# One priority number of the mixer from 40000 to 15000, and the longer lag one attention unit earlier

## The chip, the cores and the metric

The kernel runs on one core of a Trainium2 chip. The metric is the device time of one launch in microseconds (us). The launch before takes 2202.68 us (median of 3 runs, 2202.24 to 2213.45). Five engines run at the same time, each through its own list of instructions in a fixed order: TensorE (PE, matrix multiplications), VectorE (DVE), ScalarE (ACT), GpSimd (POOL) and SyncE (SP), whose list is almost only the start of transfers. An instruction that waits holds up all that stands behind it in its list. 16 DMA engines move the data.

## The reference, cut to what matters

Two layers with shared weights run over 128 context tokens and 512 latent tokens, 640 columns in one tile of 642. The reference computes, for each layer:

```
h = rmsnorm(x) * (1 + scale1) + shift1                  # modulated by c or c_ctx
aq, ak, av, bq, bk, bv, cz, cx, cb, cc, cdt, du = split(h @ w_in)
ya = diff_attention(aq, ak, av)       # 4 heads, two softmaxes each, subtracted
yb = gqa_attention(bq, bk, bv)        # 4 query heads on 2 key heads
yc = ssd_mixer(cz, cx, cb, cc, cdt)   # bidirectional state space scan in chunks of 128
yd = s5_mixer(du)                     # bidirectional complex diagonal scan, then a GLU
y  = concat(ya, yb, yc, yd) @ w_out
x  = x + gate1 * rmsnorm(y)
g, v = split(dwconv(h2 @ w_up));  x = x + gate2 * rmsnorm((silu(g) * v) @ w_down)
```

Keys, values and scan states of the context are outputs too. The four mixers of a layer do not depend on one another; each needs only its own columns of `h @ w_in`.

## The kernel before, in words

Activations lie with features on the 128 partitions and tokens in the columns. Every float32 product is made of three matmuls on parts rounded to float32r (`lin3`: high x high, high x low, low x high), over the token spans 0 to 256 and 256 to 642. A projection of 128 features is 8 chunks x 3 matmuls x 2 spans = 48 matmuls.

A layer has a mixer stage (`mixer`) and an FFN stage (`ffn`). The mixer emits, in this order of code: the first four projections (`first_proj`: du0, du1, aq0, ak0); the rest in the order of the string `ORD` (V for values and dt; bk, cz, bq, cx, aq1, ak1, cb, cc; each Q step normalises, rotates and stores queries or keys to DRAM); `ssd_steps`; `s5` (the S5 recurrence, in four quarters, each with tables `s_tb` and `s_to` loaded from DRAM into a single buffer); `s5_glu`; `ssd`; `attention`; and `w_out` in two parts. In layer 0 the modulation weights of later stages (`adaln`, tile `wm`) run between them.

What sets the order in each engine's list is not the order of the code. Each part is emitted under a priority (`self.prio`, from the table `PR`), and the scheduler takes, among the instructions that are ready by its own reckoning, the one with the smallest number. Before, the order of the numbers in a mixer is: s5 0, glu 10000, attn 20000, ssd 30000, proj 40000, st 55000, w_out 61000 and 62000. Layer 1 adds 1000000. The list of every engine is then fixed; on the chip it runs in that order whatever comes late.

`attention` has six units: heads 0 and 1 of the first differential pair, one GQA unit with two query heads, the same again. A unit is a list of (front, back) pairs. A front makes scores (`pse<-k,q`), takes maxima on DVE and exponentials on ACT (tile `at_p`, 4 buffers). A back turns the weights on PE (`psu<-identr,at_p`), splits them (`at_h`, `at_l`) and multiplies them with the values (`psv<-v,at_h`). `waiting` holds the backs that lag behind their fronts. From the fourth unit on, the weights alternate between two pools, the second of which (`au`) takes the memory that `ssd` gives back.

`ssd` needs the projections cx0, cx1, cb and cc, convolved (`cf`), and the memory of the S5 and query-key tiles, so it comes after `s5_glu`. Names in rows: `s_tb`, `s_to` S5 tables; `s_yh<-s_gs` matmuls are the GLU; `sd_...` and `cf` the SSD; `at_...` attention; `d_aq`, `d_bq`, `d_bk` queries and keys in DRAM, `q` and `k` the same loaded for a unit; `wr<-in_w_in` projection weights; `wm` modulation weights. The projections write the PSUM tile `psp` from `hh`, `hl` (activations) and `wh`, `wl` (weights).

Of the kernel before, what the change touches and what calls it, by code (L numbers as in the profile page):

```python
# [33 lines left out]
LAG = 1  # L34
# [2 lines left out]
SB = "vu"  # L37
WX = 8
XP = 0
PR = {"proj": 40000, "s5": 0, "glu": 10000, "ssd": 30000, "attn": 20000, "f0": 60000, "f1": 61000, "tab": 50000, "st": 55000, "lead": 299000, "wg": 165000, "norm": 300000, "first": 310000}  # L40
WP = (61000, 62000)
MID = 6
NTMP = (("nsr", TW - SPLIT, 2), ("nsr", TW - SPLIT, 2))
# [29 lines left out]
class K:  # L73
# [1272 lines left out]
    def attention(self, l, pool, kq):  # L1346

        self.attn_begin(l, pool)
        units = ((0, 0, 0), (0, 0, 1), (1, 0), (0, 1, 0), (0, 1, 1), (1, 1))
        waiting, new = [], self.attn_unit(l, pool, kq, *units[0])  # L1350
        self.tb, self.work = itertools.cycle("u"), itertools.cycle([pool])
        with ExitStack() as more:
            for i in range(len(units)):
                if i == 3:
                    self.tb = itertools.cycle("ud")
                    self.work = itertools.cycle([pool, more.enter_context(self.pool(f"au{l}", "right"))])
                items, new = new, self.attn_unit(l, pool, kq, *units[i + 1]) if i + 1 < len(units) else None
                for front, back in items:
                    front()
                    waiting.append(back)  # L1360
                    if len(waiting) > LAG + (i > 2):
                        waiting.pop(0)()
            for back in waiting:
                back()
# [20 lines left out]
    def ffn_first(self, l, pool, yp):  # L1385
# [4 lines left out]
        with self.pool(f"wx{l}", "right", NFIRST - 4 if WPL else 4) as wx:  # L1390
            self.leading([(self.a["w_up"][l, j], self.put(r, j % 2)) for j, r in enumerate(first)],
                         lambda i: self.pss(tags[i]), wx, 1000000 * l + PR["lead"], pool if WPL else None)
        return first
# [86 lines left out]
    def mixer(self, l, base, fill):  # L1480

        self.qd = {}
        with ExitStack() as left, ExitStack() as early:
# [8 lines left out]
            pb = proj.enter_context(self.pool(f"pj{l}"))  # L1492
            with self.pool(f"ld{l}", bufs=2) as lead, self.prio(base + PR["proj"]):
                raw = self.first_proj(l, pb, lead)
            pc = proj.enter_context(self.pool(f"pc{l}"))
            qk = early.enter_context(self.pool(f"qk{l}", "right"))
            with self.prio(base + PR["proj"]):
                sp = early.enter_context(self.pool(f"s5{l}", "right"))
                raws = {"aq0": raw[0], "ak0": raw[1]}
                self.cf = {}  # L1500
                for op in ORD.split():
# [13 lines left out]
                    else:  # L1515
                        for t in self.cz:
                            self.silu2(self.raw(pb), t, t)
            with self.prio(base + PR["st"]):
                self.ssd_steps(pb)
            with self.prio(base + PR["s5"]):  # L1520
                ys = self.s5(l, sp, pb)
            fill(0, base + PR["f0"])
            with self.prio(base + PR["glu"]):
# [287 lines left out]
```

## Time and profile before

| | us |
|---|---|
| median of 3 runs | 2202.68 (2202.24 to 2213.45) |
| the profiled execution, own time | 2191.5 |
| its span, first to last instruction | 2189.7 |
| layer 0: first S5 matmul to GLU / GLU to end of SSD | 153.5 / 122.7 |
| layer 1: first S5 matmul to GLU / GLU to end of SSD | 137.2 / 184.5 |
| attention after the SSD and first part of w_out: layer 0 / layer 1 | 118.5 / 122.0 |

The durations all come from the one profiled execution. Its own time is 11.2 us under the median of the runs, so a difference worked out in it is set against 2191.5 and then carried over to 2202.7. A stage is read by how long it lasts and by how busy PE, DVE and the transfers are in it; "granted clock" is the share of TensorE's 2.4 GHz that it was given on average, 0.5 being the lower level of 1.2 GHz.

### The profile page before, as it was taken

The numbers are of one execution on the slowest core, as the hardware profiler recorded it, in microseconds if no ns is written. First come the engines' busy times: TensorE is split into PE (matmuls) and PEld (weight loads), VectorE is DVE, ScalarE is ACT, GpSimd is POOL, SyncE is SP. The second block draws the span as 40 slices with busy tenths as digits, with TensorE's granted clock in tenths as the row PEclk, the third lists the DMA queues.
The fourth block names the chain that finished last, engine by engine and source line by source line (L and its number), as shares of the span: only waits on it lengthen the run. The fifth ranks groups of instructions, "written<-read, shape, count | busy, mean of one in ns | idle before, by whom it ended". The sixth has DMA issues, their size and how long they took to land.

```text
span 2189.7 us, 33260 instructions
## 1 busy us (share of the span) xinstructions
PE 1956.1 (89%) x12812; PEld 1786.6 (82%) x12812; DVE 1245.6 (57%) x2879; ACT 802.4 (37%) x1614; POOL 676.4 (31%) x723
## 2 busy tenths in 40 slices
PE   5996789999699999999988797897985999999997
PEld 2895775876597888999988786876875999999996
DVE  6876785475768575233366475653847631323345
ACT  3423353443452223232343244442444533313241
POOL 3553424200433352122244232323104332212232
PEclk9997789888799999999988887886866999999998
DMA  7464325134305665222224521310112012222221
GB/s 295 136 207 160 114 74 177 40 101 131 107 20 185 197 223 190 85 77 73 91 79 149 184 98 61 117 45 10 51 40 95 20 56 80 73 82 70 75 87 49
DMA packets 93511, 230.29 MB, mean 105 GB/s; under 512 B 17960, under 2 KB 30888, under 8 KB 93352
## 3 DMA queue, kind: packets, MB, share of 16 engines
q1 hardware_dynamic: 82856, 213.46, 29.8%
q10 hardware_dynamic: 10496, 14.71, 1.9%
q8 instruction: 101, 1.65, 0.3%
q14 instruction: 58, 0.48, 0.1%
HBM read 192.21 MB, written 35.92 MB: 104 GB/s over the span
## 4 chain that ended last, share of the span: by engine, by line
PE 67%; DVE 15%; DMA 9%; ACT 3%; issue 2%; POOL 2%; SPq 1%; ACTq 0%; POOLq 0%; DVEq 0%
PE psb L81 34%; PE psp L81 12%; PE psd L81 7%; PE pse L81 6%; PE psv L81 5%; DMA s_tb<-s5td 2%; DMA wm<-in_w_mod 1%; DVE nt L391 1%; PE psu L1209 1%; DMA wr<-in_w_down 1%; DVE x L394 1%; DMA ck<-in_cache_ak 1%; DVE wl L98 1%; DMA q<-d_bq 1%; DVE at_s L1279 1%
## 5 line engine op out<-in xcount | busy, mean ns | idle before, releaser
L81 PE MATMUL psb<-hh,wh 128*128 128x256 f32 (+1 forms) x1152 | 359.1, 312 | 2.3 <-DVE cv L451 2.3
L81 PE MATMUL psb<-hl,wh 128*128 128x256 f32 (+1 forms) x1152 | 358.3, 311 | 0.0
L81 PE MATMUL psb<-hh,wl 128*128 128x256 f32 (+1 forms) x1152 | 357.3, 310 | 0.0
L98 POOL TENSOR_TENSOR wl<-wr,wh 128x1024 fp32r<-128x1024 f32 (+3 forms) x87 | 192.3, 2211 | 502.7 <-ACT wh L95 451.6
L95 ACT CAST wh<-wr 128x1024 fp32r<-128x1024 f32 (+3 forms) x174 | 168.6, 970 | 417.9 <-PE psb L81 283.4
L81 PEld LDWEIGHTS psb<-hh,wh 128*128 128x128 f32 x1152 | 217.9, 189 | 13.3 <-issue 8.2
L81 PE MATMUL psp<-hh,wh 128*128 128x386 f32 (+1 forms) x640 | 215.3, 337 | 10.7 <-ACT hh L374 7.8
L81 PEld LDWEIGHTS psb<-hl,wh 128*128 128x128 f32 x1152 | 218.7, 190 | 3.4 <-issue 3.4
L81 PEld LDWEIGHTS psb<-hh,wl 128*128 128x128 f32 x1152 | 218.1, 189 | 3.4 <-issue 3.4
L81 PE MATMUL psp<-hl,wh 128*128 128x386 f32 (+1 forms) x640 | 209.8, 328 | 0.1
L81 PE MATMUL psp<-hh,wl 128*128 128x386 f32 (+1 forms) x640 | 207.0, 324 | 0.3 <-POOL wl L98 0.3
L98 DVE TENSOR_TENSOR wl<-wr,wh 128x1024 fp32r<-128x1024 f32 (+3 forms) x87 | 100.1, 1151 | 144.0 <-ACT wh L95 143.6
L81 PE MATMUL psb<-uh,wh 128*128 128x256 f32 (+1 forms) x544 | 169.9, 312 | 0.0
L81 PE MATMUL psb<-ul,wh 128*128 128x256 f32 (+1 forms) x544 | 169.4, 311 | 0.0
L81 PE MATMUL psb<-uh,wl 128*128 128x256 f32 (+1 forms) x544 | 169.1, 311 | 0.0
L81 PE MATMUL pse<-k,q 96*128 96x128 f32 (+5 forms) x288 | 107.1, 436 | 44.6 <-ACT at_p L1195 15.1
L81 PEld LDWEIGHTS psp<-hh,wh 128*128 128x128 f32 x640 | 129.0, 202 | 17.4 <-ACT hh L374 8.8
L81 PEld LDWEIGHTS psp<-hl,wh 128*128 128x128 f32 x640 | 129.3, 202 | 2.6 <-issue 1.1
L81 PEld LDWEIGHTS psp<-hh,wl 128*128 128x128 f32 x640 | 128.6, 201 | 1.4 <-issue 0.5
L1419 POOL TENSOR_TENSOR cv<-cv,cv 128x642 f32<-128x642 f32 x44 | 71.6, 1629 | 170.5 <-DVE cv L451 141.2
L81 PEld LDWEIGHTS pse<-k,q 96*128 96x128 f32 (+2 forms) x288 | 60.5, 229 | 77.7 <-issue 32.5
L450 DVE SCALAR_TENSOR_TENSOR cv<-psb,vec,cv 128x641 f32<-128x641 f32 x72 | 63.5, 881 | 103.2 <-ACT cv L449 103.2
(525 smaller groups left out, 4741.7 us busy)
## 6 DMA issues: line engine op xcount, KB each, us to landing
wm<-in_w_mod SPq DMA_DIRECT2D x96, 512.0 KB
wr<-in_w_up SPq DMA_DIRECT2D x88, 512.0 KB
wr<-in_w_in SPq DMA_DIRECT2D x30, 512.0 KB
wr<-in_w_down SPq DMA_DIRECT2D x32, 384.0 KB
wr<-in_w_down SPq DMA_DIRECT2D x32, 320.0 KB
wr<-in_w_out SPq DMA_DIRECT2D x16, 512.0 KB
s_tb<-s5td SPq DMA_DIRECT2D x8, 992.0 KB
s_to<-s5td SPq DMA_DIRECT2D x8, 768.0 KB
```

The costliest lines, as they stand in the source:

```text
L81: self.nc.tensor.matmul(out, w, x, start=start, stop=stop)
L95: nc.scalar.copy(hv, rv)
L98: e.tensor_sub(lv, rv, hv.bitcast(F32))
L391: nc.vector.scalar_tensor_tensor(t, y[c][:, t0:t1], gg[:, c, g:g + 1], r(t0, t1), op0=ALU.mult, op1=ALU.mult)
L394: (nc.gpsimd if c % 2 else nc.vector).tensor_add(xs, xs, t)
L450: nc.vector.scalar_tensor_tensor(out[:, 1:TW], x[:, 0:TW - 1], w[:, 0:1], out[:, 1:TW], op0=ALU.mult, op1=ALU.add)
L1209: nc.tensor.transpose(ps[:, 128 * j:128 * j + 128], s, self.c("ident"))
L1279: V.reduce_max(s[:, k:k + 1], ps, axis=AX.X)
L1419: G.tensor_mul(cv[0], cv[0], cv[1])
```

## The change

```
-PR = {"proj": 40000, "s5": 0, "glu": 10000, "ssd": 30000, "attn": 20000, ...}
+PR = {"proj": 15000, "s5": 0, "glu": 10000, "ssd": 30000, "attn": 20000, ...}
...
                     front()
                     waiting.append(back)
-                    if len(waiting) > LAG + (i > 2):
+                    if len(waiting) > LAG + (i > 1):
                         waiting.pop(0)()
```

The first line gives the projections a smaller number than attention; before, they had a larger one than attention and SSD. The second lets the third unit (index 2, GQA) keep two backs behind its fronts, as units four to six do already, in place of one. Nothing is computed differently; the FFN stages keep their order. The lists of the engines change in both mixers.

PE in layer 1, where the SSD begins. `psp<-hh..,hl..` with `wh`, `wl` at 128x386 are the last matmuls of a projection, `at_o` and `at_pp` belong to attention, `cf` to the SSD. Before:

```order
L81 MATMUL psp<-hh_96,wl 128x386
L81 MATMUL psp<-hh_100,wh 128x386
L81 MATMUL psp<-hl_101,wh 128x386
L81 MATMUL psp<-hh_100,wl 128x386
L1321 MATMUL psu<-identr,at_o 128x128
L1209 MATMUL psu<-identr,at_pp 128x128
L966 MATMUL psd<-identr,cf_12768 128x128 x5
L81 MATMUL psu<-v,at_h 128x128
L81 MATMUL psu<-v,at_l 128x64
L966 MATMUL psd<-identr,cf_12934 128x128 x5
```

The last three of the projections are in one block of 144 matmuls straight before these rows, and 240 matmuls of projections stand behind the first GLU matmul. The same place in the changed kernel, 19 rows behind the last GLU matmul:

```order
L81 MATMUL psp<-hh_100,wl 128x386
L1209 MATMUL psu<-identr,at_p 128x128 x4
L81 MATMUL pse<-k,q 128x128 x4
L81 MATMUL pse<-k,q 128x512
L966 MATMUL psd<-identr,cf_12604 128x128 x5
L81 MATMUL psv<-v,at_h 128x128
L81 MATMUL pse<-k,q 128x512
L966 MATMUL psd<-identr,cf_12768 128x128 x3
L81 MATMUL psv<-v,at_l 128x64
```

Now 86 matmuls of projections stand behind the first GLU matmul, 154 fewer, and the SSD follows the GLU with attention's rows among its own. At the other end, before 110 SSD rows in a row without another mixer's between them close the SSD; now 22 do.

SP in layer 1, where the first S5 tables are loaded. `d_aq`, `q` are attention's queries, `in_w_v`, `in_w_in` weights. Before:

```order
L1177 DMA ck<-in_cache_bk 128x128
L718 DMA s_csm<-s5sm 128x48
L744 DMA s_tb<-s5td 128x1984
L736 DMA s_u<-s5ud 128x8x80 x2
L746 DMA s_to<-s5td 128x1536
L1130 DMA out_new_ak<-raw 128x128
L88 DMA wr<-in_w_v 128x784
L1140 DMA d_aq_12082<-qk_lo 128x642
L88 DMA wr<-in_w_in 128x1024
L1166 DMA q<-d_aq_12082 96x1x642 x4
```

The changed kernel:

```order
L1177 DMA ck<-in_cache_bk 128x128
L1140 DMA d_aq_12082<-qk_lo 128x642
L1166 DMA q<-d_aq_12082 96x1x642
L88 DMA wr<-in_w_in 128x1024
L1166 DMA q<-d_aq_12082 96x1x642 x3
L88 DMA wr<-in_w_in 128x1024
L718 DMA s_csm<-s5sm 128x48
L736 DMA s_u<-s5ud 128x8x80 x2
L744 DMA s_tb<-s5td 128x1984
L746 DMA s_to<-s5td 128x1536
```

The first table moves from ahead of the store and loads of attention's queries to behind them and behind two weights; on PE, 109 more matmuls of projections and values stand ahead of the first S5 matmul of this layer.

SP in layer 0, where the fourth S5 table is loaded (`d_bq`, `d_bk`: queries and keys of the third unit). Before:

```order
L88 DMA wr<-in_w_in 128x1024
L1182 DMA q<-d_bq_2140 128x1x642
L1174 DMA k<-d_bk 128x1x642
L1175 DMA k<-d_bk 64x642
L1182 DMA q<-d_bq_2140 128x1x642
L226 DMA wm<-in_w_mod 128x1024
L744 DMA s_tb<-s5td 128x1984
```

The changed kernel:

```order
L88 DMA wr<-in_w_in 128x1024
L226 DMA wm<-in_w_mod 128x1024
L744 DMA s_tb<-s5td 128x1984
L746 DMA s_to<-s5td 128x1536
L1076 DMA ropet<-in_rope 128x1024
```

The four loads for the third unit move behind the table (by ten rows). In layer 0, 8 score, 9 turning and 27 value matmuls of attention move from ahead of the first GLU matmul to behind it; 8, 9 and 19 of them stand before the end of the SSD.

## Rows read from the trace of the kernel before

**Rows 1.** The page: span; busy time of PE, weight loads, DVE, ACT, POOL.
```profile
span 2189.7 us, 33260 instructions
PE 1956.1 (89%) x12812; PEld 1786.6 (82%) x12812; DVE 1245.6 (57%) x2879; ACT 802.4 (37%) x1614; POOL 676.4 (31%) x723
```

**Rows 2.** Stretches: length, busy of each engine (instructions), clock, DMA share, GB/s.
```profile
148.00:301.49 153.49, 111.21 (x832) 102.89 (x822) 115.62 (x283) 58.37 (x139) 56.45 (x71) 0.79 0.40 129
301.49:424.19 122.70, 115.54 (x746) 88.06 (x746) 69.49 (x217) 52.70 (x137) 38.45 (x47) 0.91 0.35 106
433.80:552.30 118.50, 111.86 (x626) 85.61 (x626) 76.67 (x209) 51.01 (x148) 10.18 (x10) 0.84 0.36 114
1199.40:1336.58 137.18, 114.14 (x794) 108.13 (x793) 88.88 (x203) 55.09 (x134) 48.60 (x59) 0.81 0.43 140
1336.58:1521.10 184.52, 155.44 (x964) 134.33 (x964) 97.05 (x253) 67.87 (x158) 51.62 (x58) 0.82 0.18 58
1475.58:1521.10 45.52, 34.19 (x220) 27.84 (x220) 17.06 (x40) 7.86 (x13) 17.12 (x24) 0.75 0.04 13
1391.96:1413.40 21.44, 21.44 (x146) 21.26 (x145) 14.72 (x19) 8.33 (x13) 8.74 (x7) 1.00 0.46 157
1188.41:1199.40 10.99, 10.99 (x62) 10.74 (x61) 6.81 (x10) 1.58 (x2) 4.24 (x12) 1.00 0.99 303
1528.20:1650.20 122.00, 108.44 (x564) 95.62 (x564) 79.36 (x207) 52.21 (x153) 13.29 (x11) 0.74 0.15 49
```

**Rows 3.** PE's waits from 1475.58 to 1521.10: releaser, total us, times, longest.
```profile
PE psd L81 <- DVE sd_cbm L1011: 4.8, 7, 1.0
PE psd L81 <- DVE sd_ea L1050: 3.8, 7, 0.6
```

**Rows 4.** Timeline of PE, layer 0: start, us, instruction; last attention matmuls before the SSD's end.
```profile
408.94 0.31 PE L81 MATMUL psv<-v,at_h 128*128 128x128 f32 x1
409.16 0.31 PE L81 MATMUL psv<-v,at_h 128*128 128x128 f32 x1
409.38 0.66 PE L1209 MATMUL psu<-identr,at_p 128*128 128x128 f32 x4
```

**Rows 5.** PE's waits from 1336.5 to 1476, layer 1.
```profile
PE pse L81 <- DMA q<-d_bq: 8.4, 2, 5.9
PE psu L1209 <- DVE hl L1325: 6.4, 1, 6.4
...
PE psu L81 <- DVE at_l L156: 0.7, 1, 0.7
PE psv L81 <- ACT at_h L155: 0.7, 1, 0.7
```

**Rows 6.** Chain of waits, layer 0, fourth table: start, us, what.
```profile
236.11 3.12 POOL s_mm L780 x2
239.24 14.21 DMA s_tb<-s5td
```

**Rows 7.** Timelines of SP and PE, layer 0: second table issued; its first matmul.
```profile
160.38 0.33 SPq L744 DMA_DIRECT2D s_tb<-s5td  x1
165.90 0.51 PE L81 MATMUL psd<-s_u,s_tb 128*64 128x80 f32 x9
```

**Rows 8.** Timeline of SP, layer 1, first and second table.
```profile
1190.08 0.42 SPq L744 DMA_DIRECT2D s_tb<-s5td  x1
...
1203.58 3.12 SPq L1166 DMA_DIRECT2D q<-d_aq  x4
...
1211.79 0.33 SPq L744 DMA_DIRECT2D s_tb<-s5td  x1
```

**Rows 9.** Chain of waits, layer 1, second table.
```profile
1211.79 16.70 DMA s_tb<-s5td
1228.54 3.37 PE psd L81 x40
```

**Rows 10.** Groups of PE from 1188 to 1650: scores, count, busy us, mean ns.
```profile
L81 PE MATMUL pse<-k,q 96*128 96x128 f32 (+5 forms) x144 | 54.1, 442 | 18.7 <-ACT at_p L1195 9.7 <-DMA q<-d_bq 8.4 <-ACT at_x L1270 0.6
```

More of the change, by code (lines that the diff above doesn't have):

```diff
@@ L39 @@
 XP = 0
-PR = {"proj": 40000, "s5": 0, "glu": 10000, "ssd": 30000, "attn": 20000, "f0": 60000, "f1": 61000, "tab": 50000, "st": 55000, "lead": 299000, "wg": 165000, "norm": 300000, "first": 310000}
+PR = {"proj": 15000, "s5": 0, "glu": 10000, "ssd": 30000, "attn": 20000, "f0": 60000, "f1": 61000, "tab": 50000, "st": 55000, "lead": 299000, "wg": 165000, "norm": 300000, "first": 310000}
 WP = (61000, 62000)
```

## The prediction, made before the changed kernel was run

> **What bounds the kernel now.** I read the page first. PE is busy 1956.1 of 2189.7 us and DVE 1245.6 [rows 1], so a gain has to come from stretches in which PE waits or runs at the lower clock, or from work that leaves the path. The stages of the two mixers come next, measured between the first S5 matmul, the first GLU matmul (G below), the end of the SSD and the first part of w_out [rows 2]. Two things stand out. From G to the SSD's end layer 0 takes 122.70 us, with PE busy 115.54 at a clock of 0.91; layer 1 takes 184.52, with PE busy 155.44 at 0.82, for 964 matmuls in place of 746. And both S5 stages leave PE idle: 42 us of 153.49 in layer 0, 23 of 137.18 in layer 1.
>
> Two stretches explain layer 1's extra time. From 1391.96 to 1413.40 PE does nothing but projections, 146 instructions in 21.44 us (0.147 each) [rows 2]; these give the SSD its inputs, so all of it is on the path. From 1475.58 to 1521.10 the SSD runs by itself: 45.52 us, PE busy 34.19, clock 0.75 [rows 2], and the waits in it go back to DVE's `sd_cbm` (4.8) and `sd_ea` (3.8), the recursion's own steps, with nothing of another mixer in between to fill them [rows 3]. In layer 0 the SSD is by itself only from 410.04 (end of the last turning matmuls) to 424.19, 14.15 us [rows 4].
>
> **The change, part by part.** What it says is not what it does. Its words put the projections behind attention; the number falls from 40000 below attention's 20000, and the rows of the order show them ahead. I price the order.
>
> Layer 1, G to SSD's end. 154 fewer matmuls of projections stand here: 154 x 0.147 = 22.6 us. The SSD starts straight after the GLU with attention's rows among its own, and is alone for 22 rows in place of 110. I take layer 0's 14.15 for that: 45.52 - 14.15 = 31.4. Together 54.0, so a stage of about 130.5. As a second way, 964 - 154 = 810 matmuls at layer 0's 115.54 / 746 are 125.5, and its idle 7.2 makes 132.7, which agrees. The smaller bound is 22.6 alone, if the SSD's waits are only spread out. The larger is 69: the waits of attention from 1336.5 to 1476 for `q<-d_bq` (8.4) and the one for `hl` (6.4) would go as well, 14.8 [rows 5]. I keep 54: the queries' loads start sooner, but so does everything behind them.
>
> Layer 1, before G. 109 more matmuls stand ahead of the first S5 matmul. There PE has no gap: 62 in 10.99 us, 0.177 each, at full clock with the DMA engines busy 99% [rows 2]. That is 109 x 0.177 = 19.3 us by which S5 starts later, and S5 leads to G. The other 45 of the 154 fall between the first S5 matmul and G, where PE idles 23 us; I take 0 (that idle time hides them) and keep 45 x 0.147 = 6.6 as the upper bound if it does not.
>
> Lag of the third unit. In layer 1 PE waited for turned and split weights 0.7 + 0.7 us in this stretch [rows 5]. I take 0, between -1.4 (both gone) and +1.4 (as much again, if the backs crowd the next unit). The backs are behind fronts in PE's list only; no transfer hangs on them.
>
> Layer 0. The fourth S5 table was issued at 239.24 and took 14.21 us to land, on the chain of waits [rows 6]. The second took 165.90 - 160.38 = 5.52 from its issue to its first matmul [rows 7]. The fourth now stands ahead of four loads for the third unit: 14.21 - 5.52 = 8.7 us. Also 44 matmuls of attention leave this stage, and their DVE work with them; after the SSD, attention and w_out use 76.67 / 626 = 0.122 us of DVE per matmul [rows 2], so 5.4 us of DVE leaves a stage where DVE is busy 115.62 of 153.49. I take 3.3 of it as lying on the chain, since DVE is not always what is waited for. That is -12, between 0 and -14.1. Behind G, 36 of the 44 return before the SSD's end, where PE has 7 us free: 8 scores x 0.442 [rows 10] = 3.5; 9 turnings at 0.66 / 4 = 0.165 = 1.5; 19 value matmuls, 9.5 pairs that follow each other by 0.22 [rows 4] = 2.1. Together +7.1 (0 if they all fall in the gaps). Layer 0 nets -5, between -14 and +7.
>
> SP's list in layer 1. The first table stood ahead of a store and four loads of attention's queries (1190.08 against 1203.58), and now stands behind them and two weights [rows 8]. The second table, behind those loads, took 16.70 us before the first of 40 matmuls could start [rows 9], against 5.52 in layer 0: 11.2 more. Since S5 starts 19.3 us later anyway, most of a late landing is hidden behind the matmuls put ahead of it. I take +4, between 0 (the wait stays behind those matmuls) and 22.4 (two tables, 11.2 each).
> The Trainium skill (DMA: Bandwidth & Descriptors, section Queues, rings and completion order) says that SP has one row of the queue grid and that each DMA engine consumes the descriptors of a ring in order. The trace agrees as far as it goes, with 16.70 against 5.52 us. By that rule nothing lets the moved table overtake the loads, and the sum would hold 22.4 in place of 4.
>
> What comes after the SSD (118.50 and 122.00 us) has the same work and is left as it is.
>
> Sum against the profiled execution's own time of 2191.5: -5 + (-54.0 + 19.3 + 4) = -35.7, so 2155.8. That execution is 11.2 under the median of the runs, so I predict 2167.
>
> **The rivals.**
>
> *DVE takes over (2181).* Layer 1's stage has 97.05 us of DVE. 14.7 of them lie beside the block of projections and go with it (14.72), leaving 82.3; at layer 0's share, 69.49 / 122.70 = 57%, that needs 144 us and not 130.5, so 40 is saved in place of 54 and the time is 14 higher. For it: the SSD's waits are for DVE. Against: in layer 1's last stage DVE is busy 79.36 of 122.00, a share of 65%.
>
> *The tables wait behind the loads (2185).* Both first tables of layer 1 land 11.2 us later, +22.4 in place of +4, which adds 18.4. For it: 16.70 against 5.52. Against: S5 starts 19.3 us later, and a landing that is late by less than that costs nothing. This is the rule of the skill named above.
>
> *The work only moves (2203).* The SSD's waits and the low clock stay and merely sit elsewhere; layer 1 saves 22.6 and pays 19.3 + 4, layer 0 nothing: +0.7, no change. For it: PE idles only 11.3 us in the SSD's last 45.52, and the rest of the saving in that stretch is work or clock. Against: layer 0 does the same mixture at 94% busy and 0.91.
>
> *S5 is starved of its tables (2220, slower).* If every quarter's table in layer 1 lands as late as the second did, S5 loses 4 x 11.2 = 44.8 and not 4; the fourth of layer 0 gains nothing and its stage pays the 7.1. That is 7.1 - 54.0 + 19.3 + 44.8 = +17.2. S5 alone leads to G, and the SSD cannot begin before it. It decides from the point at which G comes 47 us later (54 - 7), that is later than about 1384 in layer 1. For it: projections ahead of attention bring their weights and the q and k transfers into the same stage. Against: layer 1's stage moves 140 GB/s at a DMA share of 0.43 [rows 2], with room on average.
>
> That the change doesn't do what it says is, as far as the order goes, so; if its effect were the opposite one, attention ahead, nothing in the rows of the order would look as it does, and I give that no chance.
>
> **How the numbers follow.** The forecast gets 0.50, DVE 0.10, the tables 0.10, the moved work 0.16, the starved S5 0.14. A measurement of this kernel can tell about 0.5% (11 us) from no change, so faster is under 2191.7 and slower over 2213.7. Forecast, DVE and tables are faster: 0.70; the moved work is the same: 0.16; starved S5 is slower: 0.14. The likeliest case's own range: at best layer 0 -14.1, layer 1 -69 + 19.3, together -63.8, 2139; at worst layer 0 at +7 (12 more), the 6.6 of the 45 matmuls, and half of DVE's 14, 2193. The whole range goes 3 below the first, for lag and rounding, and up to 2206, past the moved work; what it leaves out is the starved S5.
>
> **What would show it.** Right: layer 1 from G to the SSD's end near 131 us in place of 184.5; no stretch of the SSD alone over 20 us; its first S5 matmul about 19 us later against the start of the mixer; layer 0's fourth table landing in 5 to 6 us; the stages after the SSD within 3 us of 118.5 and 122.0. Wrong: layer 1's stage from G over 160 us (the work only moved); G over 47 us later (starved S5), with waits of PE for `s_tb` over 30 us in layer 1; or layer 0's mixer longer by 7 or more, with the fourth table still at 14.

## The result, and the profile after

The changed kernel takes 2223.05 us (median of 5 runs, 2222.63 to 2232.97) against 2202.45 for the kernel before: ratio 1.012, 95% interval 1.009 to 1.015. It is slower; the forecast was 2167.

The page of the changed kernel, to be read beside [rows 1]:

```profile
span 2227.1 us, 33234 instructions
PE 1983.2 (89%) x12812; PEld 1797.8 (81%) x12812; DVE 1245.2 (56%) x2879; ACT 803.4 (36%) x1614; POOL 678.9 (30%) x723
```

The work is the same (12812 matmuls), but PE is busy 27 us longer. Where, the stages tell; columns as in [rows 2], in the order layer 0 to the first GLU matmul (G), G to the SSD's end, and the same for layer 1:

```profile
147.97:306.75 158.78, 109.11 (x783) 100.94 (x774) 106.11 (x263) 51.23 (x113) 52.38 (x68) 0.75 0.38 124
306.75:466.34 159.59, 147.29 (x784) 106.28 (x782) 81.50 (x237) 60.38 (x161) 42.26 (x51) 0.76 0.28 82
1268.85:1420.17 151.32, 124.83 (x863) 118.15 (x864) 91.38 (x196) 52.61 (x121) 54.04 (x63) 0.77 0.40 129
1420.17:1558.99 138.82, 128.81 (x773) 107.91 (x771) 86.37 (x250) 62.34 (x157) 41.53 (x50) 0.82 0.17 55
```

Against [rows 2]: layer 0 loses 5.3 us before G and 36.9 behind it (122.70 to 159.59), for only 38 more matmuls but at a granted clock of 0.76 in place of 0.91. Layer 1 gains 45.7 behind G (184.52 to 138.82), pays 14.1 before it, and its first S5 matmul comes 23.3 us later after the last down projection of layer 0. The SSD alone at the end shrank from 45.5 us to 11.7. From the SSD's end to attention's last value matmul, layer 0 takes 125.7 us (125.9 before), layer 1 122.7 (125.8). So the loss is in layer 0, and in layer 1 some 8 us are left of the gain.

What happened at the end of layer 0's S5 stage. SP's list there (start, time to issue, what):

```profile
279.92 0.56 SPq L1182 DMA_DIRECT2D q<-d_bq  x1
280.57 0.53 SPq L1174 DMA_DIRECT2D k<-d_bk  x1
281.15 5.28 SPq L1175 DMA_DIRECT2D k<-d_bk  x1
286.48 0.65 SPq L1182 DMA_DIRECT2D q<-d_bq  x1
287.77 5.81 SPq L829 DMA_DIRECT2D s_gw<-in_d_glu  x1
```

The chain of waits at the same place:

```profile
286.50 1.25 DVE s_mm L814
...
287.77 16.85 DMA s_gw<-in_d_glu
```

And PE's waits from 285 to 320:

```profile
PE pse L81 <- ACT at_pp L1195: 13.8, 1, 13.8
```

The third unit's four loads, which had stood ahead of the fourth S5 table, now stand straight ahead of the GLU's weights `s_gw`. These take 16.85 us to land. Before, the chain of waits had:

```profile
297.72 3.08 DMA s_gw<-in_d_glu
```

ACT waits for them with its cast `s_gs<-s_gw` and has attention's exponentials `at_pp` queued behind it:

```profile
304.72 0.62 ACT L832 CAST s_gs<-s_gw 128x512 fp32r<-128x512 f32 x1 [15.73 <-DMA s_gw<-in_d_glu]
305.24 0.36 ACT L1195 ACTIVATE at_pp<-pse,at_s 128x128 f32<-128x128 f32 x1
```

So PE, DVE, ACT and POOL all stand still for some 13 us: a wait "for ACT" that is a wait for a transfer. Three windows show what the queue does meanwhile. After, from 299 to 304:

```profile
299.00:304.00 5.00, 0.00 (x0) 0.00 (x0) 0.00 (x0) 0.00 (x0) 0.00 (x0) 0.50 0.13 50
```

Before, while the same four loads (first row) and four loads of a differential unit (second) were under way:

```profile
235.00:238.00 3.00, 3.00 (x24) 2.52 (x24) 2.68 (x6) 1.85 (x8) 2.67 (x2) 0.50 0.13 51
309.00:312.00 3.00, 2.58 (x11) 2.34 (x10) 1.66 (x8) 2.09 (x8) 0.00 (x0) 0.50 0.19 72
```

The DMA share is 0.13 and 0.19, as much as 2 and 3 of the 16 engines; the trace does not name the engines. The loads read `d_bq[0:2]` and `d_aq[0:3]`, tensors whose outer dimension is 2 or 3. Three loads of 321 KB at 50 GB/s are an estimated 19 to 20 us of work. That what comes behind them in the queue has to wait for the same engines is a reading; the experiments with cut loads test it.
The Trainium skill (DMA: Bandwidth & Descriptors, section Why a DMA increments its semaphore by 16 and not by 1) says that a transfer is spread over the largest number of engines, at most 16, that divides the slowest dimension other than 1 both of what it reads and of what it writes. The trace agrees: 2/16 and 3/16 are 0.125 and 0.19.

It happens a second time behind G. Four loads of the fourth unit stand at 343.15 to 346.16, and modulation weights behind them:

```profile
347.50 15.84 DMA wm<-in_w_mod
```

Before, the fourth unit's loads had no transfer behind them on SP for 12 us:

```profile
309.30 0.72 SPq L1167 DMA_DIRECT2D k<-d_ak  x1
321.76 0.34 SPq L978 DMA_DIRECT2D sd_h<-in_ssd_h  x1
```

PE's clock before and behind this place:

```profile
315.00:348.50 33.50, 30.27 (x157) 18.75 (x156) 20.95 (x63) 16.15 (x51) 8.70 (x11) 0.86 0.51 152
348.50:379.00 30.50, 26.44 (x90) 14.11 (x88) 8.73 (x30) 5.81 (x17) 3.41 (x6) 0.55 0.38 113
```

PE waited 2.4 and 1.7 us for `wm` there, ran for most of the 30.5 us at the lower level of 1.2 GHz (0.55 on average), and did 90 matmuls in 30.5 us after 157 in 33.5. Of the 36.9 us, waiting is only 5.1 (idle 12.3 against 7.2); 38 matmuls at before's 115.54 / 746 = 0.155 are 5.9; the other 26 go with the clock: PE's busy time times the granted clock is 112 us in place of 105.

A second profile of the changed kernel says how much of this belongs to the one execution.

**The changed kernel once more.** 

> The changed kernel once more, for a second profiled execution. Its times spread from 2222 to 2233, and two kernels with the same lists in layer 0 up to the SSD's end gave 148 to 151 us for the stage behind the first GLU matmul and not 158. If the waits behind the narrow loads are the cause, they return at the same places with the same lengths (GLU's weights 16 to 17 us, modulation weights behind the fourth unit's loads 15 to 17), and that stage takes 145 to 160. If the low clock of the first profile was chance, the stage falls to under 140 while the waits stay.

The stage from G to the SSD's end in the second profile:

```profile
306.82:466.49 159.67, 147.08 (x784) 106.44 (x782) 81.47 (x237) 60.32 (x161) 42.26 (x51) 0.76 0.27 82
```

2227.32 us, ratio 1.0104 (1.007 to 1.0139). The stage repeats to 0.1 us, with the GLU's weights at 16.64 and `wm` at 15.94. It isn't chance.

**The kernel before once more.** 

> The kernel before once more, for a second profiled execution: how much of the difference between two profiles is the execution and how much the kernel. From the spread of its times (2192 to 2213) stages should differ by up to 8 us from the first profile; from the first GLU matmul to the SSD's end 120 to 132 in layer 0, 178 to 190 in layer 1.

2198.27 us, ratio 1.0008 (0.9985 to 1.0032). The two stages are 119.5 and 185.0 us, 122.7 and 184.5 in the first profile. The two profiles of each kernel agree (2191.5 and 2192.6; 2228.9 and 2229.1), but lie 37 us apart where the medians lie 21 to 24 apart. The profiled executions of the kernel before lie near the lower end of its runs (2190 to 2213), those of the changed kernel in the middle of its own (2220 to 2233); so the stages show more of the loss than the medians. The stages below tell where time goes, the ratios how much.

### The profile page after: what moved, and what is told of

The parts are those of the page before. It is cut to its first block, busy times and chain, and to the rows that moved or that the text cites. A ratio compares the mean times of both kernels' runs of the same rounds, so it can differ in the third digit from the quotient of the medians.

```text
span 2227.1 us, 33234 instructions
## 1 busy us (share of the span) xinstructions
PE 1983.2 (89%) x12812; PEld 1797.8 (81%) x12812; DVE 1245.2 (56%) x2879; ACT 803.4 (36%) x1614; POOL 678.9 (30%) x723
## 4 chain that ended last, share of the span: by engine, by line
PE 65%; DVE 16%; DMA 10%; ACT 3%; issue 3%; POOL 2%; SPq 1%; POOLq 0%; DVEq 0%; ACTq 0%
PE psb L81 34%; PE psp L81 11%; PE psd L81 7%; PE pse L81 6%; PE psv L81 5%; DMA wm<-in_w_mod 2%; DMA s_tb<-s5td 1%; DVE nt L391 1%; PE psu L1209 1%; DMA wr<-in_w_down 1%; DVE x L394 1%; DVE at_s L1279 1%; DMA s_gw<-in_d_glu 1%; DMA wr<-in_w_in 1%; DMA k<-d_ak 1%
## 5 line engine op out<-in xcount | busy, mean ns | idle before, releaser
L81 PE MATMUL pse<-k,q 96*128 96x128 f32 (+5 forms) x288 | 113.3, 457 | 42.8 <-ACT at_p L1195 18.7
```

What stands on the lines that cost most here:

```text
L81: self.nc.tensor.matmul(out, w, x, start=start, stop=stop)
```

## The experiments: which edit, which layer

The theories: A, the projections' number does it, by what it puts behind attention's narrow loads in layer 0; B, the longer lag does it; C, the mixture of attention and SSD itself runs slowly, whatever the loads do.

**The projections' number alone** (this edit and the next three are against the changed kernel).

```
-                    if len(waiting) > LAG + (i > 1):
+                    if len(waiting) > LAG + (i > 2):
```

> The projections' number at 15000, the third unit's lag as before. Theory A (the projections' number does it, in layer 0, through where the loads of the third unit stand): about 2223, ratio 1.009 to 1.012, as with both edits, and ACT waits 13 to 15 us for the GLU's weights in layer 0. Theory B (the longer lag does it): about 2202, ratio 1.000.

2225.62 us, ratio 1.0103 (1.0064 to 1.0142); ACT waits 16.4 us for the GLU's weights; layer 0 behind G takes 155.1. The number alone brings about the whole loss.

**The lag alone.**

```
-PR = {"proj": 15000, ...}
+PR = {"proj": 40000, ...}
```

> The longer lag of the third unit alone, the projections' number at 40000. Theory A: 2202, ratio 0.998 to 1.002, layer 0 from the first GLU matmul to the SSD's end 122 to 124 us. Theory B: about 2223, ratio 1.01, that stage near 157.

2208.68 us, ratio 1.0047 (1.0027 to 1.0067): neither theory. The lag costs some 10 us, which the forecast had at 0. Its two stages of layer 1, before and behind G:

```profile
1224.99:1393.06 168.07, 131.94 (x933) 124.30 (x933) 107.83 (x236) 66.39 (x162) 54.00 (x62) 0.84 0.37 119
1393.06:1543.92 150.86, 123.83 (x800) 105.44 (x799) 79.09 (x220) 55.27 (x128) 47.58 (x54) 0.84 0.19 59
```

Here the projections have their old number, and still the stage behind G is 33.7 us shorter than before and the one ahead of it 30.9 longer. So most of the shorter SSD stage, which the forecast booked as the gain of the new number, comes without that number too, as a shift of the border between two stages: together they are 2.8 us shorter than before.

**The new number in layer 1 only, and in layer 0 only** (both with the longer lag; the line stands in two places, and both were changed):

```
-                base + PR["proj"]
+                base + (PR["proj"] if l else 40000)      # layer 1 only
+                base + (40000 if l else PR["proj"])      # layer 0 only
```

> Both edits, but layer 0's projections back at 40000. Theory A: layer 1 nets about -8 (GLU to SSD's end 45 shorter, start of S5 23 later, S5 stage 14 longer), layer 0 as before: 2194, ratio 0.996. Rival (layer 1 pays as much as it gains or more): 2202 or above, ratio 1.000 to 1.005. The forecast's own working for layer 1 (-31): 2171, ratio 0.986.

> Both edits, but layer 1's projections back at 40000. Theory A: all of the loss and more, 2225 to 2240, ratio 1.010 to 1.017, with layer 0's stage from the first GLU matmul to the SSD's end at about 157 and ACT's wait for the GLU's weights over 10 us. The forecast's working for layer 0 (-5): 2197, ratio 0.998.

Layer 1 only: 2213.09, ratio 1.0062 (1.0041 to 1.0084), hardly above the lag alone. The 2194 expected of theory A, with a gain of 8 us in layer 1, did not come; its rival, that layer 1 pays as much as it gains, did. Layer 0 only: 2250.01, ratio 1.0237 (1.0208 to 1.0265). The new number loses in layer 0, as expected, and more so. Layer 1, from the last down projection of layer 0 to the SSD's end, takes 383 us before, 382 with the lag alone, 380 with the number alone, 385 and 392 in these two, 375 and 372 in the two profiles of the changed kernel: six orders within 20 us of one another. The late S5 start of layer 1 isn't its own number's doing either: with the old number in layer 1 the first S5 matmul comes 92 us after the down projection, with the new one in layer 1 alone 63 (61.5 before). It goes with what the scheduler put ahead of that matmul on PE: 403 matmuls since the down projection in the kernels where it comes 84 to 92 us after it, 291 to 307 in those where it comes 60 to 63 us after it (293 before).

The stage behind G of the kernel with the new number in layer 0 only, whose lists up to there are those of the changed kernel:

```profile
307.10:456.38 149.28, 133.70 (x784) 94.67 (x782) 81.38 (x237) 60.25 (x161) 43.35 (x51) 0.85 0.29 88
```

The same 784 matmuls take 10 us less at 0.85. The lists set the waits, but not the whole of the clock; what does is open.

## The experiments: the narrow loads

**All loads cut**, in the changed kernel and in the kernel before. The same bytes, in pieces whose outer dimension is 32 or 64:

```
-    nc.sync.dma_start(q[i].bitcast(F32), self.qd[f"bq{u}"][0:2, r])
+    for j in range(2): nc.sync.dma_start(q[i][64 * j:64 * j + 64].bitcast(F32), self.qd[f"bq{u}"][j, r])
...
-    nc.sync.dma_start(q[i][0:96].bitcast(F32), self.qd[f"aq{u}"][:, f:f + 32])
+    for j in range(3): nc.sync.dma_start(q[i][32 * j:32 * j + 32].bitcast(F32), self.qd[f"aq{u}"][j, f:f + 32])
```

and the same for the keys.

> The changed kernel with attention's query and key loads cut into pieces of 32 or 64 rows (the same bytes; 3 or 2 transfers in place of each one whose outer dimension is 3 or 2). Theory A (these loads run on 2 or 3 of the 16 DMA engines, and what stands behind them on SP waits for those engines): the GLU's weights land in layer 0 in 3 to 6 us and not 16.85, PE's 13.8 us wait for at_pp goes, modulation weights behind the next four loads land in 5 us and not 15.8, the clock from the first GLU matmul to the SSD's end rises from 0.76 to 0.88 or more and the stage falls from 158 to 125 to 135; 2175 to 2195, ratio 0.988 to 0.997. Theory C (the loss is the mixture of attention and SSD itself, at a low clock, whatever the loads do): the stage stays over 150, 2210 to 2223.

> The kernel before with the same cut loads. Theory A: the fourth S5 table of layer 0 lands in 5 to 6 us and not 14.2, the second table of layer 1 in about 6 and not 16.7, PE's waits for k<-d_ak and q<-d_bq (28 us in all) shrink by half: 2165 to 2180, ratio 0.985 to 0.992. Theory C: no transfer that is on the path changes, 2195 to 2205.

Changed kernel: 2163.11, ratio to before 0.9832 (0.9801 to 0.9862), that is 60 us under the changed kernel as it was. Kernel before: 2154.58, ratio 0.9808 (0.9780 to 0.9837). Both beat both kernels by far, and by more than expected. Layer 0 from its first S5 matmul to the SSD's end takes 272.4 us in the one and 271.5 in the other; with narrow loads it was 318.4 and 276.2. The loss of layer 0 is gone, and theory C falls. The changed kernel's loads and weights on SP, now:

```profile
280.42 1.23 SPq L1182 DMA_DIRECT2D q<-d_bq  x2
283.92 2.33 SPq L829 DMA_DIRECT2D s_gw<-in_d_glu  x2
```

and ACT's casts of the weights, which waited 0.40 and 0.57 us:

```profile
286.99 0.62 ACT L832 CAST s_gs<-s_gw 128x512 fp32r<-128x512 f32 x1 [0.40 <-DMA s_gw<-in_d_glu]
288.66 0.62 ACT L832 CAST s_gs<-s_gw 128x512 fp32r<-128x512 f32 x1 [0.57 <-DMA s_gw<-in_d_glu]
```

The weights stand behind the same loads and land in 3 us. The stage behind G in this kernel:

```profile
290.63:421.54 130.91, 122.63 (x760) 90.05 (x758) 75.43 (x220) 58.02 (x152) 41.76 (x51) 0.90 0.35 100
```

And PE's waits for loads over the whole of the kernel before, first as it was, then with cut loads:

```profile
PE psd L81 <- DMA s_tb<-s5td: 16.8, 4, 7.8
PE pse L81 <- DMA k<-d_ak: 13.9, 2, 8.4
PE pse L81 <- DMA q<-d_bq: 8.4, 2, 5.9
```

```profile
PE psd L81 <- DMA s_tb<-s5td: 1.7, 1, 1.7
PE pse L81 <- DMA k<-d_ak: 1.2, 1, 1.2
```

The scheduler, which sees more transfers, also orders other instructions differently in these kernels. In the changed kernel with cut loads 291 matmuls in place of 403 stand ahead of layer 1's first S5 matmul, which comes 23.6 us earlier after the down projection; so not all of the 60 us is the width of the loads.

**Only the GQA units' loads cut**, and **only the differential units'**. With the GQA loads cut, the lists of PE, ACT, DVE and POOL are those of the changed kernel from the first instruction to the last, and SP's differs by the pieces alone. With the differential loads cut the lists change, in both layers; they are, but for two swaps of neighbours on PE, those of the changed kernel with all loads cut.

> The changed kernel with only the GQA units' query and key loads cut into pieces of 64 rows; those of the four other units stay as they are, and SyncE's list in layer 0 keeps its order. Theory A: the GLU's weights land in layer 0 in 3 to 6 us in place of 16.85, the first GLU matmul comes 9 to 13 us earlier (294 to 298), and the later waits behind the differential units' loads stay: 2195 to 2212, about half of the loss. If the loads' width is not what holds the weights, they still land in 15 us or more and the time stays at 2223.

> The changed kernel with only the four differential units' loads cut into pieces of 32 rows. Theory A: the third S5 table of layer 0 (15.9 us) and the modulation weights behind the fourth unit's loads (15.8) land in 5 to 7 us, the GLU's weights still take 12 to 17: 2180 to 2200. If the third unit's loads were all that matters, the time stays over 2215.

GQA: 2204.59, ratio 1.0022 (1.0000 to 1.0045). ACT waits 1.90 and 1.71 us for the GLU's weights and the first GLU matmul comes at 298.88, 7.9 us earlier (9 to 13 were expected). What is left uncut still shows; chain of waits, and the stage behind G:

```profile
336.41 16.91 DMA wm<-in_w_mod
```

```profile
298.88:451.19 152.31, 138.72 (x782) 100.23 (x782) 81.07 (x228) 60.12 (x161) 42.01 (x51) 0.81 0.29 86
```

Differential: 2190.69, ratio 0.9969 (0.9946 to 0.9993). Here the GLU's weights stay late, though less than the 12 to 17 us expected (issued at 284.40, cast at 295.25), the modulation weights do not, and the stage is 15 us shorter than with the GQA loads cut:

```profile
295.25 0.62 ACT L832 CAST s_gs<-s_gw 128x512 fp32r<-128x512 f32 x1 [8.18 <-DMA s_gw<-in_d_glu]
```

```profile
298.89:436.19 137.30, 128.59 (x760) 94.69 (x758) 76.96 (x216) 58.33 (x152) 41.32 (x50) 0.86 0.32 96
```

Each half takes away the wait that stands behind it and leaves the other. Two pairs of kernels differ only in the width of the GQA loads, with the lists as good as the same: the changed kernel and the first of these (2223 to 2205), and the second of these and all loads cut (2191 to 2163). In both the intervals lie apart, so the width of these loads, with no change of order, is shown to cost 19 and 28 us. For the differential loads no such pair was run: some 23 us of what the second kernel gains on the changed one are layer 1's earlier start of S5 (61 us after the down projection).

**The GLU's weights from ACT's queue**, the loads as they were:

```
-            nc.sync.dma_start(raw, self.a["d_glu"][l, :, :, 256 * i:256 * i + 256])
+            nc.scalar.dma_start(raw, self.a["d_glu"][l, :, :, 256 * i:256 * i + 256])
```

> The changed kernel with the GLU's weights started by ScalarE instead of SyncE, so that they do not stand behind the four loads of the third unit in one queue. Theory A: in layer 0 they land in 3 to 8 us, the wait of 15.7 us on ACT and of 13.8 on PE goes, the first GLU matmul comes 10 us earlier and the stage behind it keeps its waits for modulation weights: 2205 to 2215, ratio 1.003 to 1.007. If the order of one queue is not what holds them but the busy engines themselves, they land as late as before, 16 to 17 us, and the time stays at 2223.

2214.43, ratio 1.0077 (1.0051 to 1.0104). The chain of waits shows the two halves of the weights:

```profile
287.22 7.00 DMA s_gw<-in_d_glu
294.81 7.20 DMA s_gw<-in_d_glu
```

7 us each, between 3.08 and 16.85: out of SP's queue they land sooner, but not as soon as without the loads. That they still share busy engines with them fits this; it was not shown. G comes at 302.76, 4.0 us earlier than in the changed kernel, less than the 10 expected. The time as a whole says little here: the lists change, and layer 1's first S5 matmul comes 24 us earlier after the down projection. Behind G the stage takes 138.6 us in place of 159.6, although a load of modulation weights still takes 14.85; so how the 36.9 us divide among the waits, the clock and the order behind G stays open.

**All loads cut, one edit at a time:**

> All loads cut, the projections' number at 15000, the lag as before. Theory A (with wide loads the order is worth little either way): 2155 to 2170, within 0.5% of the cut loads in the kernel before (2154.6). If the new order still loses by itself, 2170 or more; if it gains once the loads are out of the way, as the forecast had it, 2130 or less.

> All loads cut, the longer lag alone. Theory A: 2150 to 2165; the loss of 0.5% that the lag had alone came through the loads and their order too. If the lag costs by itself: 2163 or more, 0.5% over 2154.6.

Number alone 2158.68, ratio 0.9801 (0.9771 to 0.9830); lag alone 2160.54, ratio 0.9829 (0.9804 to 0.9853). The four kernels with cut loads lie between 2154.6 and 2163.1 and their intervals overlap: with wide loads neither edit can be told from no change, nor can the gain of the forecast be seen. Layer 1 up to the SSD's end takes 345 to 352 us in all four, against 367 to 392 in all the kernels with every load narrow. How the lag alone lost its 0.5% wasn't taken apart; that it shrinks to an unclear 0.2 to 0.3% with cut loads points to the loads, no more.

## Why the prediction was wrong

- **The step that failed is layer 0**, "the fourth now stands ahead of four loads for the third unit: 14.21 - 5.52 = 8.7 us", with -5 as the layer's net. It measured +42 (5.3 and 36.9). PE's wait of 7.8 us for the fourth table went, as forecast (its first matmul came 8.6 us after its issue, without a wait), but PE now waited for the third, for which it had waited 0.2:

```profile
207.58 3.61 PE L81 MATMUL psd<-s_u,s_tb 128*64 128x80 f32 x48 [9.09 <-DMA s_tb<-s5td]
```

  The GLU's weights were issued 6.2 us earlier (287.77 against 293.98). But I counted only who had been moved ahead of the loads and not who was now behind them. The price stood in [rows 6, 7]: whoever stands behind them takes 14 us. It was now paid by the GLU's weights, whose landing grew by 13.8, and again by the modulation weights. With all loads cut the two orders differ by 0.9 us in layer 0.
- **"+7.1" for 36 matmuls behind G** was right as work (38 came, 5.9 us at before's rate; with all loads cut the stage is 130.9 against 124.7 in the two orders) and missed 31 us of waits and clock.
- **Layer 1** came near the forecast in its two large terms, but not in its sum: behind G -45.7 (-54), later start +23.3 (+19.3), S5 stage +14.1 (+4). Those are -8.3, not -31. The later start came by the forecast's mechanism, matmuls put ahead (403 against 293). The S5 stage did not: the +4 was for late tables, and PE's waits for `s_tb` in it fell from 8.8 us to 1.9, though the second table still landed late (16.70 before). Waits before and after, and the table after:

```profile
PE psd L81 <- DMA s_tb<-s5td: 8.8, 2, 4.7
PE psd L81 <- DMA s_tb<-s5td: 1.9, 2, 1.0
1284.94 15.25 DMA s_tb<-s5td
```

  Instead PE is busy 10.7 us longer there, with 863 matmuls in place of 794, and idle 3.5 us longer. The term that failed is "I take 0 (that idle time hides them)" for the projections that fall into this stage: its idle time, 23.0 us before and 26.5 now, hid none of the work. The ring-order rule's 22.4, the price of two late tables, is not borne out either. Nor is the reason that I gave for the -54: the lag alone brings most of it, and layer 1's length is not set by the number. That -45.7 lies near -54 is luck, as far as the runs show.
- **The lag at 0** was wrong: +0.5% with narrow loads.
- **The stages after the SSD** were within some 3 us of before (from the SSD's end to the last value matmul), and the SSD's time alone (11.7, "over 20" excluded), as forecast.
- **The rival "S5 is starved of its tables" (2220)** hit the time for the wrong place. G of layer 1 came at 1420.17, past the 1384 that I had set as its sign; but from the last down projection of layer 0 it came 37.4 us later, under the 47, and most of the rest of the shift is layer 0's loss. PE's waits for `s_tb` fell from 16.8 to 12.7 us in all, where the rival needed over 30 in layer 1. Its idea, transfers of the path behind attention's loads, was right; the GLU's weights were the ones.

## What to carry to other kernels

When a change moves a block of loads past another transfer, read the queue on both sides: what it now stands behind, and what now stands behind it. Before pricing an order of work, look for windows in which transfers are outstanding and the DMA share is 0.13 or 0.19: a few engines may be the bound, and an edit to the shape of the load (here 44 us in the kernel before and 60 in the changed one, order included) can be worth more than a change of the order. Engines that all go idle at once, with a cast of loaded weights as the named releaser, may be waiting for that load: look at the row of the cast.

## What the runs showed of the hardware that was not expected

Loads of 321 KB whose outer dimension is 2 moved at 50 GB/s together, with two engines' worth of DMA share, and loads of outer dimension 3 at 72. With the GQA units' loads cut into 64-row pieces, the stretch in which these were under way (285 to 289 us) showed a share of 0.81 and 190 GB/s:

```profile
285.00:289.00 4.00, 1.72 (x14) 1.57 (x14) 4.00 (x12) 3.48 (x10) 1.55 (x1) 1.00 0.81 190
```

Much the same short waits came with very different times at the lower clock. Behind 2.4 and 1.7 us of waiting PE stayed near 1.2 GHz for 30 us in both profiles of the changed kernel. In the kernel with the new number in layer 0 only, with the same list on PE up to there and waits of 2.2 and 1.1 us, it was back at 2.4 GHz some 10 us sooner, and did 136 matmuls in the time of 90:

```profile
348.85:379.35 30.50, 28.71 (x136) 15.39 (x138) 11.30 (x31) 6.86 (x18) 6.55 (x9) 0.68 0.39 116
```
